# Moving one scan stream's block substitution from VectorE to GpSimd

## The chip, the cores and the metric

The kernel runs on one core of a Trainium2 chip. The metric is the device time of one execution in microseconds. The profiled execution is one more execution, recorded by the hardware profiler. Five engines work beside each other, each with a queue of its own that is done in order: TensorE (PE; PEld are its weight loads), VectorE (DVE), ScalarE (ACT), GpSimd (POOL) and SyncE (SP), which here issues most of the DMAs.

## The reference, cut to what matters

Two layers over 1024 tokens of width 1024, in fp32. Layer 0 is a mixer of two halves: an RWKV-7 scan over 8 heads of 64, and a sliding-window attention over 8 heads; both come from one input projection and go through one output projection. Layer 1 is a convolution block. After each comes an MLP with a hidden width of 4096. The change touches the scan alone:

```
def step(state, inp):
    r_t, w_t, k_t, v_t, a_t, b_t = inp
    sa = jnp.einsum('bhvk,bhk->bhv', state, a_t)
    state = (state * w_t[:, :, None, :] + sa[..., None] * b_t[:, :, None, :]
             + v_t[..., None] * k_t[:, :, None, :])
    return state, jnp.einsum('bhvk,bhk->bhv', state, r_t)
```

## The kernel before, in words

The tokens are two halves of 512. Every fp32 matrix product of the model is three matmuls (L308 to L310): a weight tile `wraw` is loaded by SyncE, ScalarE rounds it to `whi` (L291), and VectorE or GpSimd writes what is left, `wlo` (L272). Each of the three has four buffers, and a tile of 128x512 serves four steps of three matmuls. In the input projection most of the `wlo` of the stretch from 76 to 420 us are made on GpSimd.

The scan is done in chunks of 64 tokens, for a pair of heads at a time: 4 pairs in 2 halves, 8 scans. In each chunk a triangular 64x64 matrix has to be inverted. It is cut into 16x16 blocks. The diagonal blocks of a scan, 64 of them, are gathered into `ac` by masks on VectorE (L661, L663), written to DRAM (L670) and read back with one block on each of 64 partitions (L702, tile `at`, a part of C). GpSimd sets the unit matrices `xi`, a part of E (L703). Then comes the substitution: 15 steps, each one multiplication (L709, C<-C,E) and one addition (L711, E<-E,C) over n x m elements with n = 15 - j, m = j + 1, each step needing the one before. L712 transposes the result, d2 (L714) and cx (L716) bring it back to 128 partitions through DRAM, and VectorE spreads it with masks into X (L718) and XT (L720). TensorE then joins the blocks by products of 32x32 (`prod`, L734), the first of them at L740, and goes on to L771, L790 and the chain over the chunks (L817).

Two streams of scans run beside each other, each with its own tiles and PSUM banks. The first (`sc0`) does pairs 1 and 3 of the first half and then all four of the second half. The second (`sc1`) does pairs 0 and 2 of the first half, and no more.

TensorE's order is written out by hand. The parts are Python generators that `weave` steps through: a generator yields how long it is to wait, in units of a clock that counts only TensorE's work (`self.clk`), and while nothing is due the base goes on (the input projection, then the output projection and the first MLP). `LAG["ZD"]`, 40.5, is the due time of the first product after the point `begun`. The base waits for "b", the end of the second stream, before the output projection (`w_out`). On the other engines the order is chosen when the program is built, by a planner with a cost model (`schedule_with_timeline_sim`, L1600); only TensorE is exempt (`manual_schedule`, L1524).

In the stretch of the two changed scans the other users of VectorE are the other stream's masks and substitution, the attention's softmax (L899 to L918) and the token scaling. GpSimd has `wlo` and, from 147 us on, the token shift of the projected columns (L557 to L564), whose tile `sh` has one buffer.

Of the kernel before, what the change touches and what calls it, by code (L numbers as in the profile page):

```python
# [12 lines left out]
ALU = mybir.AluOpType  # L13
# [15 lines left out]
LAG = dict(SHARE=2.28, RATIO=2.35, SLACK=0.306, FIRST=0.245, GRAM=2, ATT=14, ZD=40.5, YD=8, PW=1.47, first=4.33, xT=1.27, rs=0.889, cs=1.78, lora=0.6, ss=2.8, norm=7.5, gram2=2.82, turn=1.46, bon=1.76, at=1.37, prod=0.6, wu=3, mr=1.22, chain=1.27, out=0.867, att0=0.84, att2=2, vd=5.1, load=4, wout=0.5, par0=0.356, mlp=2.98, query=14, hp=1)  # L29
# [16 lines left out]
class Net:  # L46
# [523 lines left out]

    def scan(self, hf, p, r, k, v, la, gl, sset, ptag, ahead):
        nc = self.nc
        mm = nc.tensor.matmul
        tt = nc.vector.tensor_tensor
        gtt = nc.gpsimd.tensor_tensor
# [64 lines left out]
        for src, low, qq in ((tG, ak, aq), (tF, ab, bb[:, :, :, 1, :])):  # L640
            for hp in range(2):
# [13 lines left out]
                for x, dst in ((0, low), (1, qq)):  # L655
                    tt(out=dst[:, :, hp, :], in0=psv[:, :, x, :],
                       in1=self.m2[:, x:x + 1, :].to_broadcast([P, 4, 64]), op=ALU.mult)
# [13 lines left out]
        begun = self.clk  # L671
# [32 lines left out]
        x3 = xi.rearrange("g (i c) -> g i c", c=16)  # L704
        a3 = at.rearrange("g (s t) -> g s t", t=16)
        j3 = xj.rearrange("g (i c) -> g i c", c=16)
        for j in range(15):
            n, m = 15 - j, j + 1
            tt(out=j3[:, 0:n, 0:m], in0=a3[:, j, j + 1:16].unsqueeze(2).to_broadcast([64, n, m]),  # L709
               in1=x3[:, j:j + 1, 0:m].to_broadcast([64, n, m]), op=ALU.mult)  # L710
            tt(out=x3[:, j + 1:16, 0:m], in0=x3[:, j + 1:16, 0:m], in1=j3[:, 0:n, 0:m], op=ALU.add)  # L711
        nc.vector.tensor_copy(out=xt.rearrange("g (c i) -> g c i", i=16), in_=xi.rearrange("g (i c) -> g c i", c=16))  # L712
        d2 = self.dp.tile([2, 64, 256], F32, name="d2", tag="d2" + ptag)
        nc.sync.dma_start(out=d2.rearrange("n m e -> m n e"), in_=tE[0:64, :].rearrange("m (n e) -> m n e", n=2))  # L714
# [4 lines left out]
           in1=self.bd2.unsqueeze(1).unsqueeze(3).to_broadcast([P, 8, 2, 16]), op=ALU.mult)  # L719
        tt(out=G4(XT), in0=cx[:, 8:16, :].unsqueeze(2).to_broadcast([P, 8, 4, 16]),  # L720
           in1=self.bd.unsqueeze(1).unsqueeze(3).to_broadcast([P, 8, 4, 16]), op=ALU.mult)
        yield max(0.0, begun + LAG["ZD"] - self.clk)
        C3 = lambda t: t.rearrange("p (g t) -> p g t", t=32)
        xt5 = XT.rearrange("p (g e t) -> p g e t", e=2, t=32)
        B = [slice(32 * b, 32 * b + 32) for b in range(4)]
# [879 lines left out]
```

## Time and profile before

| what | value |
|---|---|
| median of 3 runs | 2380.85 us (2377.12 to 2387.97) |
| profiled execution, its own time | 2379.74 us |
| its span, first to last instruction | 2378.0 us |
| granted TensorE clock, mean | 0.992 of full speed |
| TensorE busy | 97% |
| VectorE busy | 64% |
| ScalarE busy | 44% |
| GpSimd busy | 23% |
| chain that ended last | PE 75%, DVE 15%, DMA 4%, ACT 3% |

Busy shares are means over stages with different limits. The chain follows the last instruction back to what released it, step by step. A wait is put down to the instruction whose semaphore came last.

### The profile page before, as it was taken

How to read it: one execution, taken by the hardware profiler on the slowest of the kernel's cores; microseconds unless marked ns; L12 is line 12 of the kernel's file. 1: busy time of each engine (PE TensorE's matmuls, PEld its weight loads, DVE VectorE, ACT ScalarE, POOL GpSimd, SP SyncE). 2: the span in 40 equal slices, each digit the busy share in tenths (PEclk: the TensorE clock that was granted, in tenths of full speed). 3: DMA queues.
4: the chain of work that ended last, by engine and by line, in shares of the span. 5: the costliest groups of instructions: out<-in, count | busy, mean ns of one | idle time of the engine just before them, and what ended most of it. 6: DMA issues, size and time to landing. Idle time of an engine off the chain costs nothing.

```text
span 2378.0 us, 38508 instructions
## 1 busy us (share of the span) xinstructions
PE 2308.1 (97%) x14535; PEld 1856.4 (78%) x14535; DVE 1532.2 (64%) x2563; ACT 1047.7 (44%) x1874; POOL 542.8 (23%) x477
## 2 busy tenths in 40 slices
PE   8989889989999999999999999999999999999998
PEld 6767667767777787878888888888878778888887
DVE  7775743667555464569977653799999756533334
ACT  6546634556443332443443363534433544433333
POOL 2322433110111121322000000105555422221121
PEclk9999999999999999999999999999999999999999
DMA  7345234444445454546666665563323333433332
GB/s 219 111 110 153 83 88 132 109 127 123 136 143 178 126 175 133 169 133 200 198 195 191 194 183 172 144 188 98 98 89 98 99 93 94 129 95 98 98 97 85
DMA packets 417934, 320.12 MB, mean 135 GB/s; under 512 B 44642, under 2 KB 360276, under 8 KB 417748
## 3 DMA queue, kind: packets, MB, share of 16 engines
q1 hardware_dynamic: 413684, 309.79, 43.5%
q0 software_dynamic: 2176, 4.19, 0.6%
q10 hardware_dynamic: 1888, 3.67, 0.5%
q8 instruction: 114, 1.87, 0.3%
q14 instruction: 72, 0.59, 0.1%
HBM read 257.29 MB, written 60.29 MB: 134 GB/s over the span
## 4 chain that ended last, share of the span: by engine, by line
PE 75%; DVE 15%; DMA 4%; ACT 3%; issue 2%; SPq 0%; POOL 0%; DVEq 0%; ACTq 0%; POOLq 0%
PE mm L308 23%; PE mm L309 22%; PE mm L310 22%; DVE acc L1321 5%; DMA raw<-p 1%; PE sc L734 1%; DVE C L709 1%; DVE E L711 1%; PE sc L652 1%; DVE hidl L272 1%; PE sc L817 1%; PE sc L771 1%; DMA cx<-d 1%; DVE x L1253 1%; PE at L936 1%
## 5 line engine op out<-in xcount | busy, mean ns | idle before, releaser
L291 ACT CAST whi<-wraw 128x512 fp32r<-128x512 f32 x720 | 445.7, 621 | 986.9 <-PE mm L309 890.9
L308 PE MATMUL mm<-h,whi 128*128 128x512 f32 x1792 | 725.8, 406 | 7.1 <-ACT h L383 2.4
L310 PE MATMUL mm<-h,wlo 128*128 128x512 f32 x1792 | 704.1, 394 | 1.4 <-POOL wlo L272 1.4
L309 PE MATMUL mm<-h,whi 128*128 128x512 f32 x1792 | 703.3, 393 | 1.3 <-DVE h L272 1.0
L272 POOL TENSOR_TENSOR wlo<-wraw,whi 128x512 fp32r<-128x512 f32 x302 | 422.2, 1399 | 1233.8 <-ACT whi L291 1178.5
L1321 DVE SCALAR_TENSOR_TENSOR acc<-u,par,acc 128x512 f32<-128x512 f32 x480 | 429.8, 905 | 10.0
L308 PEld LDWEIGHTS mm<-h,whi 128*128 128x128 f32 x1792 | 339.7, 190 | 89.7 <-issue 12.8
L310 PEld LDWEIGHTS mm<-h,wlo 128*128 128x128 f32 x1792 | 339.1, 189 | 75.7 <-POOL wlo L272 2.3
L309 PEld LDWEIGHTS mm<-h,whi 128*128 128x128 f32 x1792 | 340.0, 190 | 69.0 <-issue 2.4
L308 PE MATMUL mm<-hidh,whi 128*128 128x512 f32 x992 | 389.4, 396 | 0.1
L309 PE MATMUL mm<-hidl,whi 128*128 128x512 f32 x992 | 386.0, 390 | 0.9 <-DVE hidl L272 0.9
L310 PE MATMUL mm<-hidh,wlo 128*128 128x512 f32 x992 | 384.5, 390 | 0.9 <-POOL wlo L272 0.9
L272 DVE TENSOR_TENSOR wlo<-wraw,whi 128x512 fp32r<-128x512 f32 x258 | 183.5, 712 | 200.9 <-ACT whi L291 193.2
L1253 DVE TENSOR_TENSOR x<-mm,x 128x512 f32<-128x512 f32 x248 | 166.5, 686 | 85.9 <-PE mm L310 85.5
L308 PEld LDWEIGHTS mm<-hidh,whi 128*128 128x128 f32 x992 | 186.2, 188 | 43.5 <-issue 4.2
L310 PEld LDWEIGHTS mm<-hidh,wlo 128*128 128x128 f32 x992 | 186.2, 188 | 40.3 <-POOL wlo L272 1.3
L309 PEld LDWEIGHTS mm<-hidl,whi 128*128 128x128 f32 x992 | 186.3, 188 | 40.0 <-DVE hidl L272 1.3
L272 DVE TENSOR_TENSOR hidl<-rel,hidh 128x512 fp32r<-128x512 f32 x109 | 84.9, 780 | 77.9 <-ACT hidh L1230 76.5
L1232 DVE CAST hidh<-rel 128x512 fp32r<-128x512 f32 x68 | 34.2, 506 | 89.8 <-ACT rel L1226 89.6
L1226 ACT ACTIVATE rel<-rel 128x512 f32<-128x512 f32 x128 | 80.6, 633 | 3.9 <-ACT rel L1225 0.4
L1225 ACT ACTIVATE rel<-mm 128x512 f32<-128x512 f32 x128 | 75.6, 593 | 2.2 <-DVE hidl L272 2.0
L1557 POOL COPY u<-u 128x30 f32<-128x30 f32 x8 | 3.2, 399 | 250.2 <-DVE acc L1321 250.2
(377 smaller groups left out, 2191.9 us busy)
## 6 DMA issues: line engine op xcount, KB each, us to landing
wraw<-in_mlp_w_dram SPq DMA_DIRECT2D x512, 256.0 KB
lo<-wlo SPq DMA_DIRECT2D x160, 256.0 KB
wlo<-lo SPq DMA_DIRECT2D x160, 256.0 KB
wraw<-in_cv_pw_w_dram SPq DMA_DIRECT2D x96, 256.0 KB
wraw<-in_hy_w_in_dram SPq DMA_DIRECT2D x80, 256.0 KB
wraw<-in_hy_w_out_dram SPq DMA_DIRECT2D x32, 256.0 KB
p<-stg SPq DMA_DIRECT2D x30, 256.0 KB
raw<-p SPq DMA_DIRECT2D x40, 128.0 KB
```

Source lines behind the costliest of these rows:

```text
L272: return eng.tensor_tensor(out=out, in0=x, in1=hi.bitcast(F32), op=ALU.subtract)
L291: nc.scalar.copy(out=hi, in_=raw)
L308: mm(ps, lhsT=whi, rhs=xhi, start=start, stop=False)
L309: mm(ps, lhsT=whi, rhs=xlo, start=False, stop=False)
L310: return mm(ps, lhsT=wlo, rhs=xhi, start=False, stop=stop)
L652: mm(ps[64 * q:64 * q + 64, u * P:(u + 1) * P], lhsT=src[hs, c * 64:(c + 1) * 64], rhs=ar[hs, :, c, :], start=(u == 0), stop=(u == 3), ski ...
L709: tt(out=j3[:, 0:n, 0:m], in0=a3[:, j, j + 1:16].unsqueeze(2).to_broadcast([64, n, m]), in1=x3[:, j:j + 1, 0:m].to_broadcast([64, n, m]), ...
L1225: nc.scalar.activation(out=t, in_=ps, func=AF.Relu)
L1226: nc.scalar.activation(out=t, in_=t, func=AF.Square)
L1232: nc.vector.tensor_copy(out=hi, in_=t)
L1253: last = nc.vector.tensor_tensor(out=x, in0=pss[o], in1=x, op=ALU.add)
L1321: nc.vector.scalar_tensor_tensor(out=acc, in0=u[:, j:j + H], scalar=self.pv(f"dw{j}", c), in1=acc, op0=ALU.mult, op1=ALU.add)
```

## The change

In the scans of the second stream (`ptag == "sc1"`, pairs 0 and 2 of the first half) the thirty tensor_tensor instructions of the substitution are issued on GpSimd instead of VectorE. In the other six scans they stay on VectorE. In the same two scans the due time of the first product, counted on TensorE's clock from `begun`, is 48.5 instead of 40.5.

```diff
     def scan(self, hf, p, r, k, v, la, gl, sset, ptag, ahead):
         nc = self.nc
+        other = ptag == "sc1"
...
+        sub = gtt if other else tt
         for j in range(15):
             n, m = 15 - j, j + 1
-            tt(out=j3[:, 0:n, 0:m], in0=a3[:, j, j + 1:16].unsqueeze(2).to_broadcast([64, n, m]),
+            sub(out=j3[:, 0:n, 0:m], in0=a3[:, j, j + 1:16].unsqueeze(2).to_broadcast([64, n, m]),
                in1=x3[:, j:j + 1, 0:m].to_broadcast([64, n, m]), op=ALU.mult)
-            tt(out=x3[:, j + 1:16, 0:m], in0=x3[:, j + 1:16, 0:m], in1=j3[:, 0:n, 0:m], op=ALU.add)
+            sub(out=x3[:, j + 1:16, 0:m], in0=x3[:, j + 1:16, 0:m], in1=j3[:, 0:n, 0:m], op=ALU.add)
...
-        yield max(0.0, begun + LAG["ZD"] - self.clk)
+        yield max(0.0, begun + LAG["ZD"] + (8.0 if other else 0.0) - self.clk)
```

## Rows read from the trace of the kernel before

**Rows 1.** The page: busy us, share and instructions of each engine.

```profile
PE 2308.1 (97%) x14535; PEld 1856.4 (78%) x14535; DVE 1532.2 (64%) x2563; ACT 1047.7 (44%) x1874; POOL 542.8 (23%) x477
```

**Rows 2.** Busy time by stage: stretch, its length, then by engine.

```profile
core 0: us, PE busy (x) PEld busy (x) DVE busy (x) ACT busy (x) POOL busy (x), PEclk, DMA share, GB/s
...
100.00:330.00 230.00, 205.44 (x2397) 157.14 (x2395) 159.97 (x410) 124.09 (x254) 70.77 (x84) 0.98 0.40 110
330.00:411.00 81.00, 80.55 (x988) 60.98 (x987) 26.30 (x60) 31.79 (x58) 32.27 (x32) 1.00 0.35 108
```

**Rows 3.** Timeline of PE: start, duration, instruction, [idle before <-what ended it].

```profile
131.23 0.33 PE L699 MATMUL sc<-ident,ar 128*128 128x128 f32 x1 [1.97 <-DVE krv L683]
...
148.08 0.31 PE L734 MATMUL sc<-BD,E 32*32 32x32 f32 x13 [3.24 <-ACT BD L740]
...
154.90 0.38 PE L894 MATMUL at<-kh,q 128*128 128x256 f32 x1 [1.83 <-DVE mi L940]
...
284.17 0.44 PE L652 MATMUL sc<-ar,AG 64*64 64x128 f32 x4 [1.21 <-DVE ar L622]
...
298.76 0.41 PE L677 MATMUL sc<-ident,C 128*128 128x128 f32 x2 [2.79 <-DVE bb L656]
...
317.44 0.34 PE L734 MATMUL sc<-C,BD 32*32 32x32 f32 x10 [1.63 <-DVE C L743]
...
323.80 0.38 PE L734 MATMUL sc<-E,F 32*32 32x32 f32 x12 [3.91 <-DVE F L751]
```

**Rows 4.** Busy time of line L709 in 107:122.3 and 273.9:290.8, summed.

```profile
sum 32.20, DVE 9.52; mean DVE 4.76
```

**Rows 5.** The same of line L711.

```profile
sum 32.20, DVE 9.00; mean DVE 4.50
```

**Rows 6.** Timeline of DVE.

```profile
129.79 0.68 DVE L720 TENSOR_TENSOR E<-cx,bd 128x512 f32<-128x512 f32 x1
...
279.91 1.25 DVE L711 TENSOR_TENSOR E<-E,C 64x64 f32<-64x64 f32 x1
...
281.45 0.22 DVE L711 TENSOR_TENSOR E<-E,C 64x63 f32<-64x63 f32 x1
...
289.54 0.40 DVE L656 TENSOR_TENSOR aq<-sc,m 128x256 f32<-128x256 f32 x1
...
296.92 0.43 DVE L718 TENSOR_TENSOR C<-cx,bd 128x256 f32<-128x256 f32 x1 [5.14 <-DMA cx<-d]
```

**Rows 7.** Timeline of POOL.

```profile
116.09 1.29 POOL L272 TENSOR_TENSOR wlo<-wraw,whi 128x512 fp32r<-128x512 f32 x1 [6.55 <-ACT whi L291]
...
270.57 1.27 POOL L272 TENSOR_TENSOR wlo<-wraw,whi 128x512 fp32r<-128x512 f32 x1 [6.05 <-ACT whi L291]
...
279.80 1.28 POOL L272 TENSOR_TENSOR wlo<-wraw,whi 128x512 fp32r<-128x512 f32 x1 [1.73 <-ACT whi L291]
...
289.22 1.27 POOL L272 TENSOR_TENSOR wlo<-wraw,whi 128x512 fp32r<-128x512 f32 x1 [0.75 <-ACT whi L291]
```

**Rows 8.** POOL's instructions by line and shape: xcount | busy us, mean ns | idle before.

```profile
L809 POOL COPY st<-scar 128x64 f32<-128x64 f32 x4 | 1.7, 420 | 20.1 <-PE sc L841 20.1
...
L820 POOL COPY scar<-st 128x64 f32<-128x64 f32 x4 | 1.0, 243 | 2.6 <-DVE st L818 2.6
...
L151 POOL TENSOR_SCALAR_AFFINE_SELECT bd<-bd 32x1 f32<-32x1 f32 x4 | 0.7, 180 | 0.0
```

**Rows 9.** Instructions by line and shape in 0:1000, the third matmul.

```profile
L310 PE MATMUL mm<-h,wlo 128*128 128x512 f32 x595 | 237.2, 399 | 0.0
```

**Rows 10.** Timeline of PE: first products, second stream's last transposes, first of `w_out`.

```profile
142.36 0.32 PE L734 MATMUL sc<-C,BD 32*32 32x32 f32 x15
...
310.64 0.34 PE L734 MATMUL sc<-C,BD 32*32 32x32 f32 x18
...
376.70 0.27 PE L866 MATMUL sc<-ident,BD 128*128 128x128 f32 x1
...
411.31 0.40 PE L308 MATMUL mm<-mih,whi 128*128 128x512 f32 x1
```

## What was predicted

> **What bounds the kernel now.** I read the page first. TensorE is busy 2308.1 of 2378.0 us [rows 1], so all that any change of order can win is its idle time, 70 us; VectorE is at 64% and GpSimd at 23%. Next the busy time by stage: in the stretch 100 to 330 us, where both scan streams run beside the input projection and the attention, TensorE is busy 205.44 of 230, so 24.6 us are idle there; from 330 to 411 us it is busy 80.55 of 81 [rows 2]. Then TensorE's waits of over 1 us in the touched stretch, those of them that lie beside the scans' substitutions and products: seven rows that come to 16.6 us, six of them ended by VectorE and one by ScalarE [rows 3]. VectorE is thus the engine that TensorE waits for there, and it does so by the order of its queue more than by its load.
>
> The changed code runs twice: in the scan of pair 0 (substitution from 107.0 to 122.3 us) and of pair 2 (273.9 to 290.8 us), the two of the second stream. The other six scans are as they were.
>
> **What is removed.** Thirty instructions a scan leave VectorE. They take 9.52 us in line L709 and 9.00 us in line L711 over the two windows [rows 4, 5], 18.5 us together. Undisturbed such an instruction takes 0.22 us and one that meets a GpSimd tensor_tensor takes 1.25 us [rows 6], so a good part of the 18.5 us is standing, not working. None of it is TensorE time; it counts only through the waits of rows 3. Three of these I put down to this substitution or its tail: 1.97 us (L699 behind L683, which stood behind the second stream's masks and the first stream's substitution), 1.21 us (L652 behind L622, which shared the queue with the last steps of pair 2's substitution), 2.79 us (L677's buffer behind the mask L656, which stood behind L718 while that waited 5.14 us for the DMA of cx). Two more, 1.63 and 3.91 us, fall in pair 2's products while VectorE does the first stream's substitution and waits for its cx; the changed due time moves pair 2's products away from there [rows 3, 6]. Together 11.5 us are in reach. A new order moves such meetings as often as it ends them, so I take half: a gain of 5.7 us, between nothing and 11.5.
>
> **What is added on GpSimd.** The same thirty tensor_tensor instructions on 64 partitions, with n*m elements, 680 in all for each line, 1360 a scan. No row shows a small tensor_tensor on GpSimd. A 128x512 one takes 1.28 us undisturbed [rows 7]; the cheapest instruction there that reads and writes almost nothing takes 180 ns, copies of 64 columns 243 and 420 ns [rows 8]. With 180 ns as the fixed part an element costs (1280 - 180)/512 = 2.15 ns, so 2.9 us for 1360. The bounds are 30 x 0.18 + 2.9 = 8.3 us and 30 x 0.42 + 2.9 = 15.5 us a scan; I take the middle row, 243 ns: 10.2 us. This is an estimate from those rows. On VectorE the windows were 15.3 and 16.9 us long, so by itself the chain on GpSimd is no longer than before. In its queue stand wlo subtractions (1.28 us each, at 116.09 and 270.57 with waits of 6.55 and 6.05 us for ScalarE's whi in front of them [rows 7]). If the pieces of the substitution stand between the waits, two to four such subtractions add 2.6 to 5.1 us; if they stand behind a wait, 6 us more. Against the 15.3 us of now the substitution is then done between 4 us earlier (8.3 + 2.6) and 11 us later (15.5 + 5.1 + 6).
>
> **What waits for it.** The copy L712 on VectorE, the two DMAs d2 and cx, the masks L718 and L720, and TensorE's first product L734. Pair 0's masks are done at 130.5 us (L720 starts at 129.79 and takes 0.68 us) and the product runs at 142.36 us, 11.9 us later [rows 6, 10]; for pair 2 the masks start at 296.92 us and the product runs at 310.64 us. The change also puts the product's due time 8 units later, so a substitution that is late by up to 19.9 us is covered: TensorE itself will not stand at L734 for it. Without that cover each us beyond 12 would be lost twice, once a scan.
>
> L712 is another matter: it now waits for GpSimd, and everything behind it in VectorE's queue (the other stream's masks, the attention's maxima) stands with it. The nearest row is the wait of L718 for cx: VectorE stood 5.14 us and TensorE lost 2.79 us at L677 right after, a share of 0.54 [rows 3, 6]. L712 can stand 0 to 11 us a scan by the bounds above, for which TensorE loses 0 to 5.9 us. I take 3 us of standing (the middle price, 10.2 us, with five to eight us in the queue), so 1.6 us a scan, 3.3 us for both.
>
> The subtractions wlo that now queue behind thirty more instructions: TensorE's third product of a weight tile shows no wait for them at all up to 1000 us (0.0 us for 595 matmuls) [rows 9], because four buffers run ahead. Covered as long as the delay is below the lead of such a buffer; I cost it at nothing, and if it were not covered, at up to the 6 us of one wait a scan.
>
> **What is moved.** The due time of the second stream's products. TensorE's order is written by the planner's clock, which counts TensorE's own work, so 8 units are 8 us of matmuls and some 9 with the idle time in them. The work is only reordered: projection matmuls are drawn forward. The next scan of the stream starts after the first and has the same delay again, so the stream's last transposes move from 376.70 to about 395 us. The output projection may start only when the stream is done and starts at 411.31 us [rows 10]; 16 us remain, so nothing is lost. If the stream slipped by over 34 us, each further us would be one of the total.
>
> **The sum.** -5.7 + 3.3 = -2.4 us. The profiled execution took 2379.74 us (span 2378.0 us and 1.7 around it), so 2377.3 us; the median of the three timed runs, 2380.85, lies 1.1 above the profiled one, so 2378 us.
>
> **A lock instead of a relief.** In the trace a VectorE instruction with both inputs in SBUF that starts while GpSimd does a tensor_tensor lasts until that ends (L711 at 279.91 us: 1.25 us, beside wlo from 279.80 for 1.28 us), while the mask L656 at 289.54 us, one of whose inputs is in PSUM, takes its 0.40 us beside wlo at 289.22 [rows 6, 7]. So thirty more tensor_tensor instructions on GpSimd hold VectorE's SBUF work off for 8.3 to 15.5 us a scan, against 18.5/2 = 9.3 us that VectorE gets back. The gain of 5.7 us is then gone and the wait of 3.3 us stays: 2380.85 + 3.3, about 2384 us. The Trainium skill says so as a rule: in "SBUF — State Buffer", section "Who interferes with whom", VectorE and GpSimd share one pair of SBUF ports under an exclusive lock, taken by whichever instruction starts first, and a VectorE instruction with at most one SBUF input outside the two-port modes is free of it. By that rule the move frees nothing; the trace agrees as far as large instructions go, and no run here shows it for small ones.
>
> **Rivals.** First, the lock, 2384 us; against its full price speaks that the masks, which TensorE waits for at 298.76 us, read PSUM. Second, all waits in reach go, and with them those at 148.08 and 154.90 us (3.24 and 1.83 us), which lie where pair 0's products are now: 16.6 us less [rows 3], some 2364 us. For it speaks that six of seven waits hang on VectorE; against it that the first stream's substitution stays on VectorE in the same stretch. Third, slower: a head-of-line wait. GpSimd's queue holds a substitution step behind a wlo that waits for whi, which waits for TensorE to free a buffer; VectorE stands at L712 for it. With the 420 ns row (15.5 us), four subtractions (5.1 us) and both a 6.55 and a 4 us wait the substitution takes 31 us instead of 16, VectorE stands up to 15 us a scan, TensorE loses 0.54 of that, 8 us, and twice is 16 us: 2397 us. It decides from about 11 us of standing a scan on. Against it: only the dearest price with every wait gets there, and VectorE has other work to do before L712. Fourth, the substitution on GpSimd does nothing for the time and only TensorE's new order does; it is then within a few us of before, in the same class as the forecast.
>
> **How the numbers follow.** A measurement of this kernel tells a change from none at about 0.5%, 11.9 us. Forecast (with the fourth rival) 0.42, the lock 0.20: both within 0.5%, 0.62. All waits gone 0.18, faster. Head-of-line 0.20, slower. The likeliest case alone runs from 2369 (all 11.5 us gained, no wait) to 2391 us (no gain, 10 us of the 11.8 lost); the range reaches to the outer two, 2364 to 2397 us.
>
> **What would show it.** Right: 30 tensor_tensor of L709 and L711 on GpSimd a scan, at 0.25 to 0.5 us; L718 of pair 0 before 142 us; L734 of pair 0 near 151 us without a wait; mih at L308 near 411 us; fewer VectorE waits on TensorE between 280 and 325 us. Wrong: over 0.6 us an instruction, a VectorE wait at L712 over 10 us, a TensorE wait for wlo, or an idle TensorE ahead of the first mih. A TensorE idle time between 100 and 330 us outside 12 to 36 us would make the prediction wrong.

## The result and the profile after

The changed kernel takes 2391.36 us (median of 11 runs, 2388.39 to 2396.92), the kernel before 2379.93 (11 runs beside them): ratio 1.0053 [1.004, 1.0066], 11.4 us slower, where 2 us faster was forecast. The profiled execution, 2396.89 us with a span of 2395.2, is among the longer ones; what hangs on all executions is therefore read further down from their spans and clocks, not from this trace alone. Lines from 573 of the kernel before are one higher here, those from 707 on two (L734 is L736).

First the page of the kernel after: busy time, and the chain that ended last.

```profile
PE 2315.7 (97%) x14535; PEld 1859.1 (78%) x14535; DVE 1521.0 (64%) x2503; ACT 1047.7 (44%) x1874; POOL 559.0 (23%) x537
...
PE 74%; DVE 12%; ACT 2%; issue 2%; DMA 1%; POOL 1%; SPq 0%; DVEq 0%; ACTq 0%; POOLq 0%
```

Sixty instructions have gone from VectorE to GpSimd, VectorE's share of the chain fell from 15% to 12%, and the kernel is slower. TensorE's busy time rose by 7.6 us for the same 14535 matmuls [rows 1]: that is to be explained first. Busy time by stretch: start and end, length, busy time by engine, then the granted clock as a share of full speed (PEclk). Before, in other stretches than [rows 2]:

```profile
100.00:160.00 60.00, 51.12 (x598) 40.18 (x596) 47.81 (x134) 26.18 (x62) 16.04 (x16) 0.97 0.42 111
160.00:220.00 60.00, 58.16 (x847) 43.68 (x844) 36.87 (x93) 29.62 (x68) 13.06 (x23) 1.00 0.46 129
220.00:330.00 110.00, 96.16 (x956) 73.28 (x956) 75.29 (x185) 68.29 (x127) 41.67 (x45) 0.97 0.35 100
...
410.00:430.00 20.00, 20.00 (x95) 15.58 (x95) 11.55 (x19) 15.09 (x23) 3.17 (x3) 1.00 0.41 124
```

After; the fourth row, a part of the second, holds the largest loss of this execution:

```profile
100.00:160.00 60.00, 53.13 (x432) 42.31 (x431) 43.09 (x104) 28.29 (x63) 27.14 (x50) 0.99 0.45 120
160.00:220.00 60.00, 55.48 (x912) 42.42 (x911) 24.86 (x61) 19.72 (x47) 8.83 (x15) 0.83 0.38 108
220.00:330.00 110.00, 99.26 (x803) 74.07 (x802) 76.89 (x180) 74.79 (x142) 51.38 (x79) 0.98 0.34 96
...
180.00:200.00 20.00, 17.66 (x134) 13.13 (x133) 5.23 (x11) 6.93 (x13) 1.46 (x2) 0.57 0.12 35
...
410.00:430.00 20.00, 14.81 (x67) 10.89 (x67) 6.70 (x12) 6.89 (x12) 4.14 (x4) 0.88 0.36 114
```

From 160 to 220 us TensorE is idle 4.5 us instead of 1.8, and runs at a mean clock of 0.83: 0.17 x 60 = 10 us of work at full speed are missing, and no idle time shows them. At half clock (1.2 instead of 2.4 GHz) the engine counts as busy. Its waits there, and those at the end of the first half (timeline of TensorE, with the idle time before an instruction and what ended it):

```profile
132.62 0.66 PE L700 MATMUL sc<-ident,ar 128*128 128x128 f32 x4 [2.24 <-DVE krv L684]
...
158.18 0.75 PE L736 MATMUL sc<-C,BD 32*32 32x32 f32 x64
...
168.89 0.61 PE L736 MATMUL sc<-E,F 32*32 32x32 f32 x25 [1.46 <-DVE F L753]
...
181.18 0.66 PE L792 MATMUL sc<-bb,BD 64*64 64x128 f32 x8 [1.09 <-ACT BD L780]
183.09 1.12 PE L792 MATMUL sc<-bb,BD 64*64 64x128 f32 x8 [1.25 <-DVE BD L778]
...
271.58 0.80 PE L868 MATMUL sc<-ident,BD 128*128 128x128 f32 x3 [3.89 <-DVE BD L856]
...
393.99 0.60 PE L868 MATMUL sc<-ident,BD 128*128 128x128 f32 x4
...
413.97 1.12 PE L862 MATMUL sc<-lg,gup 128*128 128x512 f32 x2 [2.00 <-DVE BD L845]
...
420.66 0.39 PE L308 MATMUL mm<-mih,whi 128*128 128x512 f32 x1
...
428.46 0.56 PE L308 MATMUL mm<-mih,whi 128*128 128x512 f32 x1 [3.03 <-ACT mih L1170]
```

The waits at 168.89, 181.18 and 183.09 us are short, 1.1 to 1.5 us; at the last the records show the clock low from 183.0 to 200.1 us. That length is this execution's and not the order's: in e2 and e9 below, whose order of TensorE is the same up to here, the low clock begins at the same wait or 1.2 us behind it and lasts 6.8 us. The first `mih` comes 9.35 us late [rows 10]; the last of the output projection's 128 `mih` matmuls is 15.0 us late (3.03 of the difference at its gate, the last row), and at 1003 us the kernel is 17.45 us behind. From there on the distance to before stays within 0.4 us of the spans' 17.2.

The part that was to be watched went well. GpSimd's substitution (its timeline):

```profile
108.07 0.21 POOL L711 TENSOR_TENSOR C<-C,E 64x15 f32<-64x15 f32 x1
108.36 0.24 POOL L713 TENSOR_TENSOR E<-E,C 64x15 f32<-64x15 f32 x1
...
112.75 0.82 POOL L713 TENSOR_TENSOR E<-E,C 64x55 f32<-64x55 f32 x1
...
115.52 0.31 POOL L713 TENSOR_TENSOR E<-E,C 64x64 f32<-64x64 f32 x1
...
123.17 0.21 POOL L713 TENSOR_TENSOR E<-E,C 64x15 f32<-64x15 f32 x1
```

and what VectorE has beside and behind it (its timeline), a 64x512 instruction, the waits at the copy L714, and pair 0's mask L720:

```profile
112.70 0.69 DVE L272 TENSOR_TENSOR q<-raw,q 64x512 fp32r<-64x512 f32 x1 [0.84 <-ACT q L1025]
...
123.42 0.54 DVE L714 COPY E<-E 64x256 f32<-64x256 f32 x1 [2.18 <-POOL E L713]
...
130.94 0.42 DVE L720 TENSOR_TENSOR C<-cx,bd 128x256 f32<-128x256 f32 x1 [0.63 <-DMA cx<-d]
...
308.31 1.46 DVE L714 COPY E<-E 64x256 f32<-64x256 f32 x1 [2.58 <-POOL E L713]
```

### The profile page after: what moved, and what is told of

Read it like the earlier page. It is cut to its first block, busy times and chain, and to the rows that moved or that the text cites. A ratio compares the mean times of both kernels' runs of the same rounds, so it can differ in the third digit from the quotient of the medians.

```text
span 2395.2 us, 38477 instructions
## 1 busy us (share of the span) xinstructions
PE 2315.7 (97%) x14535; PEld 1859.1 (78%) x14535; DVE 1521.0 (64%) x2503; ACT 1047.7 (44%) x1874; POOL 559.0 (23%) x537
## 4 chain that ended last, share of the span: by engine, by line
PE 74%; DVE 12%; ACT 2%; issue 2%; DMA 1%; POOL 1%; SPq 0%; DVEq 0%; ACTq 0%; POOLq 0%
PE mm L308 23%; PE mm L309 22%; PE mm L310 22%; DVE acc L1323 5%; PE sc L736 1%; DVE hidl L272 1%; PE sc L819 1%; PE sc L653 1%; PE sc L773 1%; DVE nt L517 1%; PE at L938 0%; DVE h L272 0%; DVE x L1255 0%; PE sc L804 0%; PE sc L792 0%
## 5 line engine op out<-in xcount | busy, mean ns | idle before, releaser
L308 PE MATMUL mm<-h,whi 128*128 128x512 f32 x1792 | 725.6, 406 | 9.4 <-ACT h L383 2.4
L272 POOL TENSOR_TENSOR wlo<-wraw,whi 128x512 fp32r<-128x512 f32 x302 | 420.7, 1394 | 1183.2 <-ACT whi L291 1128.0
L308 PEld LDWEIGHTS mm<-h,whi 128*128 128x128 f32 x1792 | 339.7, 190 | 93.2 <-issue 13.2
L308 PE MATMUL mm<-hidh,whi 128*128 128x512 f32 x992 | 390.9, 397 | 1.2 <-DVE hidh L1234 1.1
L272 DVE TENSOR_TENSOR wlo<-wraw,whi 128x512 fp32r<-128x512 f32 x258 | 184.0, 714 | 200.3 <-ACT whi L291 190.0
L308 PEld LDWEIGHTS mm<-hidh,whi 128*128 128x128 f32 x992 | 186.2, 188 | 43.6 <-issue 2.3
L272 DVE TENSOR_TENSOR hidl<-rel,hidh 128x512 fp32r<-128x512 f32 x109 | 83.7, 768 | 79.4 <-ACT hidh L1232 78.2
```

The lines of the kernel that those rows point to most:

```text
L272: return eng.tensor_tensor(out=out, in0=x, in1=hi.bitcast(F32), op=ALU.subtract)
L308: mm(ps, lhsT=whi, rhs=xhi, start=start, stop=False)
```

## The experiments

Each is an edit of the changed kernel. All were run in five rounds beside the kernel before, whose median was 2377.8 to 2380.6 us in the five sessions. The last two columns are means over all timed executions: span x (1 - mean granted clock), the time lost to a lower clock, and the rest of the span, which holds work at full clock and waiting. (Waiting at the low clock is counted half in each, and the clock is known to 0.001, some 2 us, in one execution.)

| kernel | GpSimd | due | median us | ratio to before | lost to clock | rest |
|---|---|---|---|---|---|---|
| before | no | 0 | 2379.9 | 1 | 22 to 25 | 2352 to 2355 |
| after | sc1 | +8 | 2391.4 | 1.0053 [1.004, 1.0066] | 28.5 | 2362.2 |
| e1 | sc1 | 0 | 2370.8 | 0.996 [0.9946, 0.9974] | 18.2 | 2350.5 |
| e2 | no | +8 | 2406.2 | 1.011 [1.0095, 1.0125] | 39.4 | 2363.8 |
| e12 | sc1, longer | 0 | 2374.3 | 0.9983 [0.9971, 0.9995] | 20.2 | 2351.8 |
| e4 | all 8 scans | 0 | 2377.3 | 0.9987 [0.9976, 0.9997] | 24.7 | 2350.4 |
| e7 | first half, 4 scans | 0 | 2378.4 | 0.9993 [0.9982, 1.0003] | 24.8 | 2351.1 |
| e3 | sc1 | -6 | 2386.5 | 1.0032 [1.002, 1.0045] | 24.7 | 2360.9 |
| e14 | sc1 | -3 | 2389.7 | 1.0043 [1.003, 1.0056] | 26.7 | 2359.8 |
| e15 | sc1 | +1 | 2367.7 | 0.9959 [0.9945, 0.9972] | 18.9 | 2347.7 |
| e8 | sc1 | +3 | 2385.8 | 1.0032 [1.0018, 1.0047] | 26.0 | 2357.7 |
| e16 | sc1 | +16 | 2404.9 | 1.0114 [1.01, 1.0129] | 37.9 | 2366.0 |
| e5 | sc1 | +8, pair 0 | 2387.9 | 1.004 [1.0027, 1.0053] | 28.6 | 2358.6 |
| e6 | sc1 | +8, pair 2 | 2379.0 | 1.0 [0.9989, 1.0011] | 20.2 | 2357.7 |
| e9 | sc1 | +8, gate order | 2383.7 | 1.0022 [1.0012, 1.0032] | 24.2 | 2358.9 |
| e10 | sc1 | 0, gate order | 2375.2 | 0.9987 [0.9976, 0.9997] | 20.8 | 2352.6 |
| e11 | sc1 | +8, both streams | 2388.9 | 1.005 [1.0034, 1.0067] | 26.7 | 2360.8 |
| e13 | sc1 | +8, sc0's pair 1 | 2399.3 | 1.0087 [1.0073, 1.0101] | 30.6 | 2366.9 |
| e17 | no | as e13 | 2392.7 | 1.0052 [1.0037, 1.0068] | 26.3 | 2364.7 |
| e18 | no | as e14 | 2392.4 | 1.0055 [1.004, 1.007] | 27.9 | 2362.3 |

**The two halves of the change (e1, e2).** e1 leaves out the due time, e2 the engine.

```diff
-yield max(0.0, begun + LAG["ZD"] + (8.0 if other else 0.0) - self.clk)
+yield max(0.0, begun + LAG["ZD"] - self.clk)                            # e1
-sub = gtt if other else tt
+sub = tt                                                                # e2
```

> Substitution of the second stream on GpSimd, its due time as before (40.5), so TensorE's order is that of before. Order theory (the loss comes from the later due time: it lets the first stream and the attention slide, their work then misses the start of the output projection): within 5 us of before, ratio 0.998 to 1.002; first mih matmul near 411 us. Engine theory (the loss comes from GpSimd: lock on VectorE, GpSimd's queue): 8 to 14 us slower, ratio 1.0035 to 1.006. Clock theory (the long stretch at half clock behind 183 us in the trace of the changed kernel makes most of it, and it follows from TensorE's order there): as the order theory.

> Substitution on VectorE as before, due time of the second stream 8 later; TensorE's order is that of the changed kernel. Order theory: as the changed kernel, 8 to 14 us slower, ratio 1.0035 to 1.006, first mih after 418 us and a wait of 2 to 4 us for the third k of the first stream behind it. Engine theory: within 4 us of before. If both parts count, between the two.

GpSimd alone gains 9.8 us, the due time alone costs 25.6, together they cost 11. In the traces TensorE's instructions stand in the same order in e1 as before, and in e2 as after. So the engine was a gain and the due time the whole loss. Both sizes were missed: the order theory had e1 within 5 us of before and e2 at 8 to 14 us, though e2's signs, the first `mih` after 418 us (426.31) and a wait behind it (3.03 us), are there. The means split the loss: from e1 to after 10.3 us more are lost to the clock and 11.7 us in the rest, from before (beside it) to e2 some 15 and 10. They split e1's gain as well: some 6 us of it are clock and 3 the rest. Windows of e1, which answer to those above:

```profile
100.00:160.00 60.00, 53.01 (x605) 41.69 (x603) 42.65 (x107) 25.65 (x57) 24.28 (x46) 0.97 0.43 112
160.00:220.00 60.00, 58.08 (x852) 43.59 (x844) 36.37 (x92) 30.58 (x73) 13.14 (x23) 1.00 0.46 129
220.00:330.00 110.00, 100.92 (x1023) 76.90 (x1025) 66.14 (x157) 69.38 (x129) 52.83 (x79) 0.97 0.37 105
...
410.00:430.00 20.00, 20.00 (x99) 15.46 (x97) 12.09 (x22) 14.04 (x21) 3.00 (x3) 1.00 0.48 137
```

Between 100 and 160 us 1.9 us of idle time are gone against before, between 220 and 330 us 4.8; the clock in these windows is as before, and the first `mih` comes 5.34 us earlier.

**More GpSimd (e12, e4, e7).** e12 is e1 with each multiplication issued twice; e4 and e7 are e1 with more scans on GpSimd.

```diff
+for _ in range(2 if other else 1):          # e12, around the multiplication
-sub = gtt if other else tt
+sub = gtt                                   # e4
+sub = gtt if hf == 0 else tt                # e7
```

> GpSimd for the second stream, due time as before, and each of the 15 multiplications issued twice (the second writes the same values again): 15 more GpSimd instructions a scan, some 5 us. If the substitution's length on GpSimd is covered by the time to the product (masks of pair 0 end some 12 us ahead of it) and the shared ports cost little at this size, 2371 to 2375 us, with VectorE standing up to 5 us longer at the copy behind it. If GpSimd's time is paid through held VectorE work or that copy, at 0.54 of it for two scans, 2376 to 2382 us.

> All eight scans substitute on GpSimd, due times as before, TensorE's order as before. Engine theory: four times the price of the two scans, 30 us or more slower, with VectorE standing at the transposing copy behind GpSimd. Order theory with a cheap GpSimd (a step takes 0.2 to 0.3 us there by the trace of the changed kernel, as on VectorE): within 8 us of before.

> GpSimd for all four scans of the first half (both streams), due times as before, the second half on VectorE. If the gain comes from relieving VectorE where it is crowded: 0 to 6 us faster than the second stream alone, ratio 0.9935 to 0.996. If two substitutions and the weight remainders in one GpSimd queue hold each other up: 0 to 8 us slower than it, ratio 0.996 to 0.9995.

Fifteen more GpSimd instructions a scan cost 3.5 us by the medians and 5.5 by the ratios (the intervals overlap): most of the substitution's length is covered, as forecast. With the first stream's scans on GpSimd too, 6.5 to 7.6 us of the gain are lost again, and by the means all of that is clock (24.7 and 24.8 against 18.2) with the rest as in e1. The traces show where. VectorE's queue in e4, then TensorE:

```profile
319.95 1.45 DVE L714 COPY E<-E 64x256 f32<-64x256 f32 x1 [5.32 <-POOL E L713]
326.71 0.42 DVE L720 TENSOR_TENSOR C<-cx,bd 128x256 f32<-128x256 f32 x1 [5.31 <-DMA cx<-d]
...
327.77 0.69 DVE L778 COPY BD<-sc 128x512 f32<-128x512 f32 x1
...
328.51 0.90 PE L792 MATMUL sc<-bb,BD 64*64 64x128 f32 x9 [6.59 <-DVE BD L778]
```

Pair 3's copy waits for GpSimd and its mask for the DMA behind it, and pair 2's L778, whose product TensorE had finished at 319.04 us, stands in the same queue behind both. TensorE, matmul for matmul 7.7 us ahead of e1 at 320 us, waits 6.59 us, its clock is low from 323.9 to 341.0 us, and at 350 us it is 4.4 us behind e1. In e7 the same wait is 7.25 us, the clock is low for 17.1 us as well, and TensorE goes from 10.5 us ahead to 2.7 behind. So in both traces moving more of the same work gains until one wait in VectorE's queue takes more than that back.

**The dose (e3, e14, e15, e8, e16).** Only the 8.0 changes: -6, -3, 1, 3, 16.

```diff
-(8.0 if other else 0.0)
+(1.0 if other else 0.0)                     # e15; -6.0 e3, -3.0 e14, 3.0 e8, 16.0 e16
```

> GpSimd for the second stream and its due time 6 EARLIER than before (34.5). In the trace of before pair 0's masks were done 11.9 us ahead of the product, so 6 us less are still covered. Order theory: the second stream ends earlier and so do the first and the attention; first mih not later than before; 0 to 8 us faster than before, ratio 0.9965 to 1.0. Engine theory: slower than before by 8 us or more, as GpSimd's part stays. Covered margin wrong: a wait of several us of TensorE at the first product, slower.

> GpSimd for the second stream, its products due 3 units earlier. If lateness is what is paid, earlier costs nothing of itself, and the loss at 6 units earlier (2386.5 us) would be from TensorE waiting for the masks, which at 3 units still end some 9 us ahead: 2368 to 2376 us. If any shift of the order costs about the same: 2380 to 2390 us.

> GpSimd for the second stream, its products due 1 unit later; some 800 lines of TensorE's order differ, against over 5000 for 3 or 8 units. A price by units says 2 to 5 us over 2371, 2373 to 2376 us; a price by whether the order changes much says near 2371 us too, up to 2376; a price by any change at all says over 2380 us.

> As the changed kernel, with the added due time at 3 units instead of 8. If the price of the due time grows with it, as a delay would, the gain of GpSimd alone (2371 us) loses 3/8 of the 21 us between that and the changed kernel: about 2379 us. If it is a matter of which steps meet in TensorE's order, the price need not grow with the units: anything between 2368 and 2392 us, and it should be read from the waits: 2370 to 2374 us if TensorE's wait at the masks of L736's score tile near 169 us (1.46 us) and the half clock near 183 us are missing, over 2385 us if they are there.

> GpSimd for the second stream, its products due 16 units later. If lateness is what is paid, twice the units cost clearly more than 8 units (2391 us): the streams end some 35 us later than in the kernel before, the gate stands for them, 2400 to 2420 us. If any shift costs about the same, 2382 to 2395 us.

Against e1 the price is +16, +19, -3, +15, +21 and +34 us for -6, -3, +1, +3, +8 and +16. Three units in either direction cost nearly as much as eight; one unit costs nothing (e15 and e1 are not told apart). Nor does the price follow how much of the order changes: of TensorE's 14535 places (by line, names and shape, in the traces) another matmul than before stands in 696 with 1 unit, in 1664 with 3 (the expectation has over 5000), 3804 with -3, 6062 with 8 and 6182 with -6.

Earlier products are not covered to the full: in e3 TensorE stands 2.09 us at pair 2's first product for its mask (299.46 us), in e14 it does not. Twice the eight units cost 14 us more, inside the range forecast for a price of lateness, but by the means 9 of the 14 are clock and the wait at the gate is the same 3.03 us; that lateness by itself is paid for is not shown. e8 missed its forecast: the wait near 169 us and the half clock near 183, without which it should have taken 2370 to 2374 us, were not there, and it loses in other places (1.69 to 2.98 us at 242, 248, 250 and 327 us). So it is not one meeting that costs; each of these orders has its own.

**One pair at a time (e5, e6).**

```diff
-(8.0 if other else 0.0)
+(8.0 if other and p == 0 else 0.0)          # e5; p == 2 in e6
```

> GpSimd for the second stream, the due time 8 later in pair 0 alone. Between the GpSimd part alone (0.996 of before) and the whole change (1.0053) lie some 21 us. Crowding theory (the later products of pair 0 fall on the first stream's and the attention's small matmuls at 160 to 200 us; TensorE waits there and its clock falls): most of it is here, 12 to 21 us over the GpSimd part alone, ratio 1.001 to 1.005, with half clock between 160 and 200 us. Gate theory (the first stream comes too late for the output projection): a half slide costs little, under 5 us over the GpSimd part alone. Chance meetings (any other order costs about the same): 10 us, ratio near 1.0.

> GpSimd for the second stream, the due time 8 later in pair 2 alone. Crowding theory: little, 0 to 6 us over the GpSimd part alone, ratio 0.996 to 0.9985, and no half clock between 160 and 200 us. Gate theory: under 5 us too, but the rest of the loss would then come only with both. Chance meetings: 10 us, ratio near 1.0.

Pair 0's eight units cost 17 us, pair 2's 8. The first is what crowding forecast, with its sign, low clock from 170.2 to 173.6 and 183.9 to 190.7 us; the second is nearer to the 10 us of chance meetings, although e6 changes 4774 places of the order and e8, which costs 15 us, 1664. Pair 0's delay is felt by the first stream as well: its pair 3 begins at 276.2 us in e5 and 279.7 after, against 260.0 in e1, although its own due times are as they were. In e6 the wait of 3.03 us at the gate of the output projection is there, as in after.

**The gate (e9, e10).** In the output projection the attention's blocks are set ahead of the first stream's late block; e9 with the due time, e10 without.

```diff
-groups = (("s2", (0, 1, 2)), ("s3", (3,)), ("att0", (4, 5, 6, 7)))
+groups = (("s2", (0, 1, 2)), ("att0", (4, 5, 6, 7)), ("s3", (3,)))
```

> The changed kernel with one edit: the output projection takes pair 3's part (which waits for the first stream) after the attention's parts instead of before them, 24 matmuls later. Gate theory: the wait of 3.0 us at the second k of it goes, and with it its stretch at half clock; 4 to 10 us faster than the changed kernel, ratio to before 1.001 to 1.0035. Crowding theory: the gate is worth its own wait at most, 1 to 5 us, ratio 1.003 to 1.005.

> GpSimd for the second stream, due time as before, and in the gate the attention's blocks set ahead of the first stream's late block, as in the run that gave the changed kernel 7.7 us back. If that gave back the wait of 3.03 us at the gate (with the fall of the clock behind it), which the kernel with GpSimd alone does not have, nothing is left to win: 2368 to 2374 us. If the new order in the gate is better by itself, another 5 to 8 us: 2363 to 2366 us.

e9 gives back 7.7 us of the changed kernel's 11.4, as the gate theory forecast: the wait at the gate and the low clock there are gone, and the means put 3.3 us of it in the rest and 4.3 in the clock. e10 does not gain but costs 4.4 against e1, with a new wait of 3.23 us (L308 behind L1194) in its trace, which is the longest of its 12 executions. The order is worth something only where the gate stands.

**Both streams later (e11).**

```diff
-(8.0 if other else 0.0)
+(8.0 if hf == 0 else 0.0)
```

> GpSimd for the second stream, and 8 units later for the products of all four first-half scans, so that both streams keep their distance. If the loss is from the second stream's products meeting the first stream's steps (crowding), it should mostly go although all scans end later: 2372 to 2381 us, with the first gate matmul later than in the changed kernel (420.7 us) by up to 10 us. If lateness itself is paid, because fewer input projection matmuls are left to put between dependent steps, it costs at least as much as in the changed kernel: 2390 to 2405 us.

Neither forecast fits. Its time lies just under that of lateness, but its profiled execution (2383.28 us, its shortest) has its first `mih` at 406.5 us, not later than before, and loses behind that, at the same wait of 3.03 us. Inconclusive.

**Another scan, and its order without GpSimd (e13, e17, e18).** e13 puts the 8 units on the first stream's pair 1; e17 and e18 are e13 and e14 with `sub = tt`.

```diff
-(8.0 if other else 0.0)
+(8.0 if not other and hf == 0 and p == 1 else 0.0)
```

> GpSimd for the second stream with its due time as before, and the 8 units on the first stream's pair 1 instead. If the loss belongs to the second stream's products being put among the first stream's steps, this shift, which parts the two streams further, costs little: 2368 to 2377 us. If any shift of this size leaves a favourable order, it costs as much as the others did (15 to 21 us over 2371): 2382 to 2392 us.

> The order of TensorE of the run with 8 units on the first stream's pair 1 (2399 us), all substitutions on VectorE. There VectorE stood 7.3 us at the copy behind GpSimd's last step and the copy took 5.25 us, and TensorE then waited 10.6 us. If these belong to GpSimd's substitution in this order, the wait goes and the time falls by 6 to 11 us: 2388 to 2393 us. If GpSimd's gain of some 10 to 15 us holds in every order, VectorE's own substitution costs it again: 2405 to 2414 us.

> The order of TensorE of the run with 3 units earlier (2390 us), all substitutions on VectorE. If GpSimd's part depends on the order, the wait of 5.2 us at 293 us (VectorE at the copy for 3.6 us, the copy 4.1 us) goes and the time is the same or lower: 2384 to 2390 us. If GpSimd's gain holds in every order: 2398 to 2406 us.

e13 is dearer than either forecast, and there GpSimd is to blame for a part: the same order without it (e17) is 0.35% faster, as forecast, and the intervals do not touch. In e13 VectorE stood 7.34 us for GpSimd, then its copy took 5.25 us (timeline of VectorE; the copy of the other stream took 0.37):

```profile
293.58 5.25 DVE L714 COPY E<-E 64x256 f32<-64x256 f32 x1 [7.34 <-POOL E L713]
```

because GpSimd's last steps stood between `wlo` and the token shift, and four 128x512 instructions followed (its timeline):

```profile
290.35 0.24 POOL L713 TENSOR_TENSOR E<-E,C 64x28 f32<-64x28 f32 x1
290.55 1.28 POOL L272 TENSOR_TENSOR wlo<-wraw,whi 128x512 fp32r<-128x512 f32 x1
...
293.33 0.21 POOL L713 TENSOR_TENSOR E<-E,C 64x15 f32<-64x15 f32 x1
293.51 1.29 POOL L564 TENSOR_TENSOR stg<-stg,sh 128x512 f32<-128x512 f32 x1
294.76 1.28 POOL L272 TENSOR_TENSOR wlo<-wraw,whi 128x512 fp32r<-128x512 f32 x1
...
296.13 1.25 POOL L272 TENSOR_TENSOR wlo<-wraw,whi 128x512 fp32r<-128x512 f32 x1
297.35 1.25 POOL L564 TENSOR_TENSOR stg<-stg,sh 128x512 f32<-128x512 f32 x1
```

TensorE paid for it (its timeline; the second row is the same place in e17):

```profile
306.53 0.87 PE L653 MATMUL sc<-ar,AG 64*64 64x128 f32 x5 [10.63 <-DVE ar L623]
...
304.89 0.69 PE L653 MATMUL sc<-ar,AG 64*64 64x128 f32 x4 [3.53 <-DVE ar L623]
```

In e18 against e14 no difference can be told; e18 lies between its two forecasts, and the wait of 5.20 us that e14 has at 293 us does not go but is 7.56 us long (292.60 us), so GpSimd was not its cause. GpSimd's part is thus worth -0.4% in the order of before, -0.6% with +8, nothing that can be told at -3, and +0.35% in e13's order.

## Why the prediction failed, point by point

**The step that failed** is the one under "What is moved": "The work is only reordered", "16 us remain, so nothing is lost". It was costed at nothing; alone it measured 25.6 us on VectorE and 20.6 on GpSimd. Its local arithmetic was right: the second stream's last transposes were forecast at about 395 us and ran at 393.99. Wrong was what I left out. The first stream was taken as fixed, and it slid by up to 20 us (its pair 3 begins at 279.7 us, at 259.9 before). The 16 us were counted to a gate that also waits for the first stream, whose last transposes ran at 424.83 us instead of 409.49, and the gate itself opened late, at 420.66 us, and stood. And a new order was priced by whether it must wait for its own inputs, not by what it does to the waits of all the others; e17 and e18 show that two more orders, with nothing on GpSimd, cost 12 to 15 us as well. Of eleven orders with a moved due time, e9's among them, only the one with 1 unit and the one with pair 2 alone are not slower than before, and the latter lost e1's gain. That 2391 us lies inside the 2364 to 2397 stated is luck: the ends of that range were set by other mechanisms.

**The frame failed with it**: "all that any change of order can win is its idle time, 70 us". The test I named, idle time outside 12 to 36 us between 100 and 330 us, was passed (230 - 207.88 = 22.1 us, from the trace of after) and the kernel was slower all the same, since 5 of 13 us by the means over all executions (in the profiled one some 9 of 17) are clock. Idle time and lost clock have to be added up.

**What is removed** had the right sign and was too small: 5.7 us forecast net of new meetings, 9.8 measured net of everything in e1. Of the five waits in reach four no longer stand in e1 (284.17, 298.76, 317.44 and 323.80 us); the one behind L683 stayed, 3.31 us in e1 and 2.24 after, so it was wrongly put down to this substitution, and e1 has a second of its kind, 3.64 us at 306.70 us [rows 3].

**What is added** held: 0.21 to 0.32 us an instruction undisturbed, against 0.25 to 0.5 forecast; 15.3 us for pair 0's substitution including the `wlo` between its steps, as long as on VectorE. VectorE stood 4.8 us at L714, 6 forecast. The mask of pair 0 was started at 130.94 us, before 142; the `wlo` kept its cover, TensorE's waits for GpSimd's are 2.3 us over the run in both traces. In e13's order the cover did not hold to the full: there TensorE waits 1.25 us for a `wlo` (289.00 us).

**The product of pair 0** was forecast near 151 us and ran at 158.18, without a wait: other due work stood ahead of it.

**The rivals.** The lock did not decide: e1 is faster by 0.4%. Small GpSimd instructions hold VectorE little: in e1's trace the 24 VectorE instructions that overlap them and nothing else on GpSimd took 10.7 us, against 10.4 by the medians of the same lines and shapes with GpSimd still. Where the two meet it was rather GpSimd's that stood: L713 of 64x55 took 0.82 us beside VectorE's L272 (112.70 us) and 0.30 at 118.19 us. Large ones hold VectorE fully [rows 6, 7], and in e13 four in a row held its copy. The rule of the Trainium skill ("SBUF — State Buffer", "Who interferes with whom"), that the shared ports are held for a whole instruction and the other engine blocks, agrees with a 64x256 copy that took 5.25 us beside four GpSimd instructions and 0.37 us elsewhere. The head-of-line rival came to 2397 us, near what was measured, but not by its mechanism: VectorE's longest wait at L714 was 2.58 us after. Waits of that kind did come in e13 (7.34 us) and in e4 and e7 (5.32 and 6.58 us), the one in e13 behind `wlo` and token shift that wait for nothing themselves. The fourth, that only TensorE's order acts, was right that the order acts, gave it the wrong size ("within a few us of before"), and was wrong that GpSimd does nothing.

What stays open: why one order keeps TensorE's clock up and its neighbour does not. Each fall between 100 and 560 us in these traces lies at a wait of 0.8 us or more among small matmuls, or shortly behind it, but the waits that are followed by one and those that are not are not told apart by any row here. One pair shows it. Up to 310 us TensorE has the same order in e1 and e6, and the same wait of 3.64 us; from 300 to 315 us e1's clock falls to a mean of 0.77, e6's stays at 1.00, at the same busy time (the wait, then the window; e1 first):

```profile
306.70 0.47 PE L700 MATMUL sc<-ident,ar 128*128 128x128 f32 x1 [3.64 <-DVE krv L684]
...
300.00:315.00 15.00, 11.36 (x246) 8.70 (x242) 8.77 (x36) 3.95 (x7) 3.69 (x5) 0.77 0.53 141
...
305.08 0.44 PE L700 MATMUL sc<-ident,ar 128*128 128x128 f32 x2 [3.64 <-DVE krv L684]
...
300.00:315.00 15.00, 11.36 (x53) 9.09 (x52) 10.67 (x34) 5.40 (x9) 6.44 (x6) 1.00 0.38 107
```

So what one trace loses to the clock at one place is in part chance, and only the means over executions are put down to an order here.

## What to carry to other kernels

Where TensorE's order is written out, a later due time is not free because its own inputs are early: ask which other chains it pushes back, and add the time lost to a lower granted clock to the idle time when you price it. When a change has an engine part and an order part, run them apart before you keep or drop it: here the better kernels, e1 with 0.996 [0.9946, 0.9974] and e15 with 0.9959 [0.9945, 0.9972], not told apart, keep the engine and drop all or seven of the eight units. A gain from moving work between engines belongs to the order it was measured in; measure it again when the order changes. And look at what stands in the queue behind an instruction that waits for the other engine: behind L714 it was pair 2's L778 in e4 and e7, and TensorE waited 6.6 and 7.3 us for it.

## What the runs showed of the hardware

A small tensor_tensor costs little more on GpSimd than on VectorE: 0.21 us for 64x15 and 0.31 for 64x64, against 0.17 and 0.22, while a 128x512 one takes 1.28 us. In a dependent chain the steps follow at 0.29 to 0.39 us there (108.07 and 115.52 us after) and at 0.20 to 0.25 on VectorE, some half again as long; pair 0's whole substitution took 15.3 us on either, with other work between the steps. And one VectorE instruction can stand through several GpSimd instructions in a row, not only the one it meets (5.25 us at 293.58 us in e13).
